# RWKV-7 block: the decay's copies to GpSimd, the inverse's transpose in two portions, and three edits to the order

## The chip, the cores and the metric

The kernel runs on one core of a Trainium2 chip. The metric is the device time of one execution in microseconds (us). Before the change it is 1290.84 us, the median of three runs (1290.55 to 1292.97).

A core has five engines, each with its own queue of instructions that it takes in order: TensorE (PE, matmul; its weight loads are shown apart as PEld), VectorE (DVE), ScalarE (ACT), GpSimd (POOL) and SyncE (SP), which here only issues DMAs. They wait for one another through semaphores. Matmuls write to PSUM, eight banks; all else lies in SBUF.

## The reference

Two layers over an input of 512 tokens by 1024 channels: an RG-LRU block with a gated convolutional FFN, then an RWKV-7 block with another. The change touches the RWKV-7 block alone:

```python
def _rwkv7_scan(r, w, k, v, aa, bb):
    ...
    def step(S, inp):
        r_t, w_t, k_t, v_t, a_t, b_t = inp
        sa = jnp.einsum('bhij,bhj->bhi', S, a_t)
        S = S * w_t[:, :, None, :] + sa[..., None] * b_t[:, :, None, :] + v_t[..., :, None] * k_t[..., None, :]
        y = jnp.einsum('bhij,bhj->bhi', S, r_t)
        return S, y
...
    decay = jnp.exp(-jnp.exp(w))
    a = jax.nn.sigmoid((a0 + (xa @ a1) @ a2).astype(f32))
    kk = (kf * k_k).reshape(bsz, seq, RWKV_H, RWKV_N)
    kk = kk / jnp.maximum(jnp.linalg.norm(kk, axis=-1, keepdims=True), 1e-12)
    kf = kf * (1.0 + (a - 1.0) * k_a)
    y = _rwkv7_scan(rh, hs(decay), kh, vh, -kk, kk * ah)
```

There are 16 heads of 64 channels. The state S of a head is 64 by 64 and depends on every token before.

## The kernel before

**Matmul precision.** Each float32 product is three matmuls (L54): both operands are split in a high part, rounded to the fast type, and a low part, the rest. For a weight, ACT makes the high part `wh` (L94) and DVE the low part `wl` (L97), each over 128x1024, some 1.0 and 1.2 us. For the mixed inputs `mix`, DVE makes both parts. Weights come by DMA, issued by SP.

**The scan in chunks.** The 512 tokens are cut into 8 chunks (NC) of 64 (C). Inside a chunk the recurrence becomes products of 64x64 matrices and the inverse of a triangular one. Blocks of 128 channels hold two heads; there are two groups of four blocks, g (or H) = 0 and 1.

- `prepare(g)` takes the decays, k and a of each block to the scaled operands. `pinv` (L1169) and `ppad` (L1172) are exponentials of the decays summed over the chunk, in the two directions, made by ACT. `ppad` is padded by one column per chunk and lies in two buffers, used in turn by the blocks. The r part of the tile AR is filled from `ppad` (L1183, 128x512): by ACT for g = 0, by DVE for g = 1. The last column of each chunk, the chunk's whole decay, goes to PC (L1187, 128x8), by ACT. DVE makes `kp` (L1180), the products with it (L1181, L1185, L1186), and ACT `sq` and `fac` (L1170, L1171). Then the norms of kk: `ssq` (L1179, PE), transposed as `sst` (L1194), reciprocals on DVE (L1198), transposed back as `rec` (L1202), split by ACT and DVE (L1204, L1205), spread to the channels by `knb` (L1211, PE) and multiplied in (L1212, DVE).
- `solve(H)` inverts the triangular 32x32 corners of all chunks at once. `aab` (L1281, PE) makes the corner matrices, DVE transposes them to A (L1294; in the second inverse A and its products D share a tile, shown as `DA`), POOL makes the identity X (L1297, L1298), and 31 steps of two DVE operations each (L1302, L1304) substitute. The result is transposed twice by DVE: to LT (L1307, 128x1024) and to XN (L1309). POOL copies LT's halves (L1313, L1314). `m1p` (L1328) and `ltp` (L1338), small PE products, complete it to 64x64.
- `rwkv_chunks` runs the steps over the chunks: masked products W (`s`, L1418, and L1425), `pe` (L1462), U from the inverse (`pu`, L1487; copied out by ACT, L1494), transposes of the keys (`tr`, L1432), the state (`pd`, L1481 and L1500), its decayed copy `tu` (L1507, DVE) and the output `py` (L1490, L1511).

**What sets the order.** The functions are generators. A projection calls `background(n)` after each small piece of its matmuls, and this advances a lane of generators by n visits, that is to their next `yield`. In the scan, `fill(i)` does the same from a table. The instructions that result are then ordered for each engine by a list scheduler with priorities and modelled durations; each engine executes in that order. `keep_in_program_order` (in `step` through `chained`) pins an instruction directly behind the one written before it on its engine. A `yield` more or less so moves what follows by one visit, and an operation given to another engine changes the order on both.

## Time and profile before

| | |
|---|---|
| time, median of 3 runs | 1290.84 us (1290.55 to 1292.97) |
| profiled execution | 1291.05 us, span 1289.3 us |
| busy: PE, DVE, ACT, POOL | 1264.2, 928.1, 642.8, 133.6 us |
| mean granted clock of PE | 0.997 |
| RWKV stage: prepare(0), first inverse, second inverse, rest of the scan | about 607 to 636, 650 to 705, 705 to 744, 744 to 890 us |

The profile is one execution. A row of the timeline has the start in us from the span's start, the time in us, the engine, line, operation, output and inputs, shapes, a count where equal instructions follow one another, and in brackets the time for which the engine had been idle and what ended it. Matmuls are pipelined: the time of one is longer than the distance to the next.

### The profile page before, as it was taken

How to read it: one execution, taken by the hardware profiler on the slowest of the kernel's cores; microseconds unless marked ns; L12 is line 12 of the kernel's file. 1: busy time of each engine (PE TensorE's matmuls, PEld its weight loads, DVE VectorE, ACT ScalarE, POOL GpSimd, SP SyncE). 2: the span in 40 equal slices, each digit the busy share in tenths (PEclk: the TensorE clock that was granted, in tenths of full speed). 3: DMA queues.
4: the chain of work that ended last, by engine and by line, in shares of the span. 5: the costliest groups of instructions: out<-in, count | busy, mean ns of one | idle time of the engine just before them, and what ended most of it. 6: DMA issues, size and time to landing. Idle time of an engine off the chain costs nothing. (4 is left out here: it accounts for less than half of the span.)

```text
span 1289.3 us, 22401 instructions
## 1 busy us (share of the span) xinstructions
PE 1264.2 (98%) x9259; PEld 1067.0 (83%) x9259; DVE 928.1 (72%) x1412; ACT 642.8 (50%) x1006; POOL 133.6 (10%) x206
## 2 busy tenths in 40 slices
PE   9999999999999999999899999999999999999998
PEld 8777888989898888877678888778889898988886
DVE  5998678757575766788999967778766566666653
ACT  6797455434343443559844346545644334343432
POOL 3000001010101010010002145410010101010100
PEclk9999999999999999999999999999999999999999
DMA  7312335455454544422212122132344454545431
GB/s 222 111 55 94 98 122 108 150 112 159 103 164 98 170 95 116 144 79 82 79 41 87 52 62 84 44 99 82 116 96 161 101 170 92 178 84 179 100 131 65
DMA packets 117829, 141.37 MB, mean 110 GB/s; under 512 B 10138, under 2 KB 91748, under 8 KB 117600
## 3 DMA queue, kind: packets, MB, share of 16 engines
q1 hardware_dynamic: 100528, 122.44, 29.8%
q0 software_dynamic: 16624, 16.47, 8.4%
q8 instruction: 72, 1.18, 0.4%
q10 hardware_dynamic: 576, 1.05, 0.2%
q14 instruction: 29, 0.24, 0.1%
HBM read 135.41 MB, written 4.52 MB: 109 GB/s over the span
## 5 line engine op out<-in xcount | busy, mean ns | idle before, releaser
L97 DVE TENSOR_TENSOR wl<-raw,wh 128x1024 fp32r<-128x1024 f32 (+1 forms) x161 | 194.4, 1213 | 124.7 <-ACT wh L94 104.0
L94 ACT CAST wh<-raw 128x1024 fp32r<-128x1024 f32 (+1 forms) x161 | 165.9, 1043 | 195.2 <-PE acc L54 56.0
L54 PE MATMUL accG<-xs,wh 128*128 128x512 f32 x448 | 138.7, 391 | 0.0
L54 PE MATMUL accU<-xs,wh 128*128 128x512 f32 x448 | 138.6, 391 | 0.0
L54 PE MATMUL acc<-hid,wh 128*128 128x512 f32 x384 | 119.8, 395 | 0.0
L744 DVE TENSOR_TENSOR lo<-raw,hi 128x1024 fp32r<-128x1024 f32 x70 | 85.5, 1222 | 39.4 <-PE accU L54 32.0
L743 ACT CAST hi<-raw 128x1024 fp32r<-128x1024 f32 x70 | 73.6, 1052 | 60.7 <-PE accU L54 25.3
L54 PEld LDWEIGHTS accG<-xs,wh 128*128 128x128 f32 x448 | 83.7, 188 | 17.3
L54 PEld LDWEIGHTS accU<-xs,wh 128*128 128x128 f32 x448 | 83.7, 188 | 17.2
L54 PE MATMUL accG<-xs,wl 128*128 128x512 f32 x224 | 87.3, 390 | 0.0
L54 PE MATMUL accU<-xs,wl 128*128 128x512 f32 x224 | 87.3, 390 | 0.0
L54 PEld LDWEIGHTS acc<-hid,wh 128*128 128x128 f32 x384 | 71.3, 187 | 16.7
L54 PE MATMUL accA<-xt,hi 128*128 128x256 f32 x480 | 83.4, 277 | 0.0
L54 PE MATMUL acc<-xs,wh 128*128 128x512 f32 x256 | 81.1, 398 | 0.0
L690 DVE SCALAR_TENSOR_TENSOR cv<-gpad,pv,cv 128x512 f32<-128x512 f32 x96 | 69.1, 748 | 12.3 <-ACT cv L688 11.8
L845 PE MATMUL acc<-wl,hid 128*128 128x512 f32 (+1 forms) x200 | 77.2, 386 | 0.0
L844 PE MATMUL acc<-wh,hid 128*128 128x512 f32 (+1 forms) x200 | 77.0, 385 | 0.0
L843 PE MATMUL acc<-wh,hid 128*128 128x512 f32 (+1 forms) x200 | 76.7, 383 | 0.0
L168 POOL DMA_DIRECT2D raw<-in_ffn_w_up_dram x20 | 25.7, 1285 | 480.8 <-DMA raw<-in_ffn_w_up_dram 336.3
L54 PE MATMUL acc<-hid,wl 128*128 128x512 f32 x192 | 75.0, 395 | 0.0
L54 PEld LDWEIGHTS accA<-xt,hi 128*128 128x128 f32 x480 | 73.2, 188 | 0.9
L54 PE MATMUL accA<-xt,lo 128*128 128x256 f32 x240 | 66.3, 276 | 0.0
(411 smaller groups left out, 2943.1 us busy)
## 6 DMA issues: line engine op xcount, KB each, us to landing
raw<-in_ffn_w_up_dram SPq DMA_DIRECT2D x106, 512.0 KB, 3.7
raw<-in_ffn_w_down_dram SPq DMA_DIRECT2D x48, 512.0 KB, 3.9
raw<-in_ffn_w_up_dram POOLq DMA_DIRECT2D x30, 512.0 KB, 5.9
raw<-in_rwkv_w_rkv_dram SPq DMA_DIRECT2D x24, 512.0 KB, 3.7
raw<-in_lru_w_in_dram SPq DMA_DIRECT2D x16, 512.0 KB, 4.3
raw<-in_lru_w_out_dram SPq DMA_DIRECT2D x8, 512.0 KB, 3.7
raw<-in_rwkv_w_out_dram SPq DMA_DIRECT2D x8, 512.0 KB, 3.6
xd<-x SPq DMA_DIRECT2D x8, 256.0 KB, 2.0
```

The source lines that it names most:

```text
L54: mm = lambda *a, **kw: self.nc.tensor.matmul(ps, *a, skip_group_check=more, **kw)
L94: put = (self.nc.vector.tensor_copy if dve else self.nc.scalar.copy)(hi, src)
L97: self.nc.vector.tensor_tensor(lo, src, hi.bitcast(F32), ALU.subtract)
L168: self.nc.gpsimd.dma_start(raw, more, accum_op=ALU.add)
L690: nc.vector.scalar_tensor_tensor(cv, pair.gp[:, e, j : j + T], cw(j), cv, ALU.mult, ALU.add)
L743: nc.scalar.copy(hi, f[p])
L744: tt(lo, f[p], hi.bitcast(F32), ALU.subtract)
L843: nc.tensor.matmul(ps, hh[:, s], wh[:, k, m], start=kk == 0, stop=False)
L844: nc.tensor.matmul(ps, hl[:, s], wh[:, k, m], start=False, stop=False)
L845: nc.tensor.matmul(ps, hh[:, s], wl[:, k, m], start=False, stop=kk == blocks - 1)
```

## The change

Five edits.

- The copies of r (L1183) and of the decay column (L1187) in `prepare` go to GpSimd for both groups: eight copies of 128x512, of which ACT made four and DVE four, and eight of 128x8, which ACT made.
- One more `yield` stands between `rec` and the `knb` loop.
- The transpose to LT is made in two halves of 16 columns; in the second inverse (H = 1) a visit lies between them.
- In the first inverse (H = 0) two visits instead of one lie between POOL's copies and `m1p`.
- In `step`, the second of U's two copies is pinned behind the first.

```diff
-                (nc.vector.tensor_copy if g else nc.scalar.copy)(rr, pp[:, :, :, 1:])
+                nc.gpsimd.tensor_copy(rr, pp[:, :, :, 1:])
                 self.done.add(("r", b))
                 nc.vector.tensor_tensor(Lc, ko, pp[:, :, :, 0:C], ALU.mult)
                 nc.vector.tensor_tensor(ko, bytok(kp), bytok(fac), ALU.mult)
-                nc.scalar.copy(PC[:, b, :], pad[:, :, C])
+                nc.gpsimd.tensor_copy(PC[:, b, :], pad[:, :, C])
                 yield 1
...
             nc.vector.tensor_tensor(rec[32:40], pr[32:40], rec[32:40].bitcast(F32), ALU.subtract)
+            yield 1
             yield 1
             for j in range(4):
...
-        nc.vector.transpose(LT[:, :, 0:32].rearrange("p u t -> p t u"), X)
+
+        for c in range(2):
+            nc.vector.transpose(LT[:, :, c * 16 : c * 16 + 16].rearrange("p u t -> p t u"), X[:, c * 16 : c * 16 + 16])
+            if H and c == 0:
+                yield 1
...
-        for _ in range(4 if H else 1):
+        for _ in range(4 if H else 2):
             yield 1
...
-            for g, bs, H, c, c2, q in gs:
+
+            for n_, (g, bs, H, c, c2, q) in enumerate(gs):
                 bh = half(1 - q)
-                nc.scalar.copy(uv[bh, bs], flat(pu[bh]))
+                chained(n_ == 0, nc.scalar.copy(uv[bh, bs], flat(pu[bh])))
```

Lines of the kernel after the change are one to six higher than before. What the edits move is best seen in three places.

ScalarE in `prepare(0)`, the difference of the two orders ( - is before, + is after). `wh` is the high part of a weight, `mt` a product for the mixed inputs.

```order
 L1169 ACTIVATE pinv<-AR_4902 128x512
-L1183 COPY AR_4902<-ppad_5254 128x4x2x64
-L1187 COPY PC<-ppad_5254 128x8
-L962 ACTIVATE mt<-x,om 128x512
 L1172 ACTIVATE ppad_5255<-AR_4902 128x8x64
 L94 CAST wh_5334<-raw_5262 128x1024
-L1171 ACTIVATE fac<-BK_4904,oka,pv 128x512
 L1170 ACTIVATE sq<-BK_4904,pv 128x512
 L1149 CAST back<-back 40x512
+L962 ACTIVATE mt<-x,om 128x512
 L1170 ACTIVATE sq<-BK_4904,pv 128x512
```

The two copies ahead of the cast are gone from this queue (two more pairs stood further ahead), and a multiplication for `mt` and a `fac` come behind the cast.

TensorE at the end of `prepare(0)`, the difference. `acc` are the projection's sums, `rec` and `knb` the norm's products.

```order
+L54 MATMUL acc_5261<-mix,wl_5398 128x512
 L1202 MATMUL rec<-ident,n_5218 40x128 x4
-L54 MATMUL acc_5261<-mix,wl_5398 128x512
-L1211 MATMUL knb<-rec,back 128x512 x4
+L1212 MATMUL knb<-rec,back 128x512 x4
 L54 MATMUL acc_5506<-early_4897,wh_5403 128x512 x2
```

The one matmul that stood between `rec` and `knb` stands ahead of both now.

VectorE at the end of the second inverse, before:

```order
L1304 TENSOR_TENSOR X<-X,DA 128x31
L1307 STREAM_TRANSPOSE LT_7154<-X 128x32x32
L1425 TENSOR_TENSOR W<-s,masks 128x512 x2
L97 TENSOR_TENSOR wl_6901<-raw_6646,wh_6900 128x1024
L1507 TENSOR_TENSOR tu<-pd,decay 64x256 x2
```

and after:

```order
L1305 TENSOR_TENSOR X<-X,DA 128x31
L1310 STREAM_TRANSPOSE LT_7155<-X 128x16x32
L1430 TENSOR_TENSOR W<-s,masks 128x512 x2
L97 TENSOR_TENSOR wl_6902<-raw_6647,wh_6901 128x1024
L1310 STREAM_TRANSPOSE LT_7155<-X 128x16x32
L1513 TENSOR_TENSOR tu<-pd,decay 64x256 x2
```

W stands behind half of the transpose instead of all of it, and the other half stands between the low part and `tu`. In the first inverse the first half moves up into the substitution, behind its step on 9x23 columns, and the second half stands where the whole transpose stood, with XN directly behind it. GpSimd's queue has the sixteen copies of `prepare` ahead of the identity of the first inverse; for its other work it keeps its order, but LT's copies of the second inverse stand behind the copies for one more step. On ACT, U's two copies stand next to each other in both orders.

## The prediction

> **What bounds the kernel now.** I read the page's first part, then TensorE's waits in the RWKV stage (600 to 890 us, the only stage that the change touches), then the windows and the timeline around the waits.

> ```profile
> span 1289.3 us, 22401 instructions
> PE 1264.2 (98%) x9259; PEld 1067.0 (83%) x9259; DVE 928.1 (72%) x1412; ACT 642.8 (50%) x1006; POOL 133.6 (10%) x206
> PE acc L54 <- ACT wh L94: 3.5, 2, 3.0
> PE pe L1462 <- DVE tu L1507: 2.6, 4, 1.1
> PE tr L1432 <- DVE W L1425: 1.5, 1, 1.5
> PE m1p L1328 <- DVE XN L1309: 1.2, 1, 1.2
> PE knb L1211 <- DVE rec L1205: 1.2, 1, 1.2
> ```

> TensorE (PE) is busy 1264.2 of 1289.3 us, so no change that leaves its matmuls as they are can win more than the 25 us that are left. The change adds and removes no matmul. It can win only the waits listed (columns: us in total, times, longest), some 10 us, and a slow clock that one of them brings. The profiled execution took 1291.05 us, 0.2 us over the median of the runs, 1290.84. The sum is made against 1291.05. A measurement of this kernel tells 0.2%, 2.6 us, from no change.

> ```profile
> 610.00:620.00 10.00, 6.98 (x27) 5.24 (x26) 10.00 (x18) 10.00 (x21) 0.00 (x0) 0.86 0.26 92
> 618.00:619.00 1.00, 1.00 (x4) 0.80 (x3) 1.00 (x2) 1.00 (x3) 0.00 (x0) 0.50 0.02 8
> 710.00:740.00 30.00, 28.17 (x548) 26.00 (x551) 27.97 (x68) 11.74 (x23) 3.35 (x9) 1.00 0.16 52
> 744.00:790.00 46.00, 45.59 (x1086) 41.91 (x1090) 31.29 (x48) 27.31 (x58) 23.27 (x33) 1.00 0.19 56
> ```

> The columns are length, busy time of PE, weight load, DVE, ACT and POOL, then the granted clock. In prepare(0), at 610 to 620, ACT and DVE are both busy for all 10.00 us while PE does 6.98. GpSimd (POOL) does nothing there. At 710 to 740 DVE, busy 27.97 of 30, carries the substitution. From 744 PE is full.

> **Part 1, r and the decay column to GpSimd.** PE's rows in prepare(0), and those of the engines that it waits for:

> ```profile
> 613.55 0.40 PE L54 MATMUL acc<-mix,wl 128*128 128x512 f32 x1
> 616.97 3.25 PE L54 MATMUL acc<-mix,wh 128*128 128x512 f32 x7 [3.02 <-ACT wh L94]
> 620.02 0.63 PE L54 MATMUL acc<-mix,wl 128*128 128x512 f32 x1
> 633.12 1.21 PE L1211 MATMUL knb<-rec,back 40*128 40x512 f32 x4 [1.16 <-DVE rec L1205]
> 615.89 1.03 ACT L94 CAST wh<-raw 128x1024 fp32r<-128x1024 f32 x1
> 614.13 0.60 ACT L1183 COPY AR<-ppad 128x512 f32<-128x512 f32 x1
> 614.64 0.20 ACT L1187 COPY PC<-ppad 128x8 f32<-128x8 f32 x1
> 614.74 0.72 ACT L962 ACTIVATE mt<-x,om 128x512 f32<-128x512 f32 x1
> 617.32 1.22 DVE L97 TENSOR_TENSOR wl<-raw,wh 128x1024 fp32r<-128x1024 f32 x1
> 627.95 0.20 DVE L1196 TENSOR_SCALAR n<-sst 128x32 f32<-128x32 f32 x1 [0.87 <-PE sst L1194]
> 630.47 0.41 DVE L1183 COPY AR<-ppad 128x512 f32<-128x512 f32 x1
> 630.80 0.69 DVE L1185 TENSOR_TENSOR AR<-BK,ppad 128x512 f32<-128x512 f32 x1
> 632.38 0.68 DVE L1205 TENSOR_TENSOR rec<-rec 8x512 fp32r<-8x512 f32 x1 [0.56 <-ACT rec L1204]
> ```

> PE stands 3.02 us for the weight's high part, which ACT casts at 615.89. Then the clock is halved: the row for 618 to 619 grants 0.50, and seven matmuls take from 616.97 to 620.02, 0.436 us each, twice their time at full clock: 1.5 us lost there and a little behind it, 1.6 in all. On ACT three r copies and three PC copies go from ahead of the cast (the last pair is quoted: 0.51 us to the next start, and 0.10), and one mix multiplication (the row at 614.74, 0.63 to the next) moves behind it: 3 × 0.61 + 0.63 = 2.5, so the cast starts near 613.4. That would cut the 3.02 to about 0.7.

> But what is late next is DVE. After eight high matmuls at 0.22 us PE needs the low part (L97), some 1.8 us after the cast's end at 614.5, and DVE has no gap up to it: of its work ahead, two operations (0.60 to the next start each, such as L1185) move behind it, so it starts at 617.32 − 1.2 and is ready about 617.3, some 1 us after PE asks. Further on, the rec row decides: knb follows rec directly in the new order, and rec is made on DVE. So the term is where L1205 starts. From 632.38 go three r copies that DVE no longer makes (0.33 of pitch each, 630.47 to 630.80) and two waits, 0.87 and 0.56, that an earlier PE closes: 632.38 − 1.0 − 1.4 = 629.95. knb came 0.74 behind L1205, so it would stand at 630.7 instead of 633.12: **2.4 us won if GpSimd's copies cost DVE nothing.** PE's other waits in this stretch are inside that number, because PE comes back to DVE's pace at knb.

> What do they cost DVE? No 128x512 copy on POOL is in this trace, so bounds come from its neighbours:

> ```profile
> L1441 POOL COPY tu<-x 64x256 f32<-64x256 f32 x32 | 16.0, 499 | 27.3 <-ACT x L1380 8.8 <-DVE XN L1309 5.4 <-DVE wl L97 4.7
> L1438 POOL COPY rts<-AR 64x128 f32<-64x128 f32 x32 | 12.5, 391 | 30.7 <-PE py L1490 18.3 <-PE pu L1487 11.1
> 714.39 0.39 POOL L1441 COPY tu<-x 64x256 f32<-64x256 f32 x1
> 781.06 1.73 POOL L1438 COPY rts<-AR 64x128 f32<-64x128 f32 x2
> 783.22 1.20 POOL L1441 COPY tu<-x 64x256 f32<-64x256 f32 x2
> 782.55 1.60 DVE L1565 TENSOR_TENSOR pr<-AR,BK 128x512 f32<-128x512 f32 x2
> 734.41 1.28 DVE L1565 TENSOR_TENSOR pr<-AR,BK 128x512 f32<-128x512 f32 x2
> ```

> From 64x128 to 64x256 a POOL copy grows by 108 ns per 128 elements of a row. Alone, as at 714.39, 64x256 takes 0.39; with 0.22 for 256 elements more, 128x512 takes some 0.6, an estimate. The engines also hold each other up: the pair L1565 takes 1.60 us beside POOL's copies (the two at 783.22 and the end of those at 781.06) and 1.28 without, so 0.32 us for two copies of 64x256, as many elements of a row as one r copy has. Six r copies stand ahead of rec, the four of block group 0 and two of group 1: 6 × 0.32 = 1.9. For the 128x8 copies I take 0.03 each, 0.2 for six (between nothing and 0.09). Then knb comes at 630.7 + 2.1 = 632.8, and **part 1 wins 0.3 us**. Bounds: 2.4 where a copy delays nothing, and where it holds DVE for its whole time, 6 × 0.6 = 3.6 and 0.1 for the small ones, the end is 634.4, a loss of 1.3. The value lies where it does because DVE has no gap at 610 to 620 in which a hold could hide. For the four copies that DVE made itself, 0.33 goes and 0.32 comes.

> [...]

> The clock should not fall again, since the longest new wait, 1 to 2 us, is shorter than the 3.02 that halved it; if it does, 1.6 is lost (third rival). What follows knb: the first product of the inverse (aab) now stands in four pieces between the projection's matmuls instead of three, and the four L1212 products run behind a low part and a mix multiplication, later by some 1.4 us of DVE: 0.1 lost, 0 to 0.4.

> **Extra visit ahead of knb, and the pin of U's copies.** rec and knb had one matmul between them and now have none, so the extra yield moves nothing that knb could hide behind: 0, with 0.23 (one matmul) as the end on the other side. U's copies already stood side by side on ACT, in that order: 0, and nothing queues anew.

> **First inverse's products one visit later.**

> ```profile
> 703.97 0.28 PE L1251 MATMUL acc<-wh,mix 128*128 128x256 f32 x1
> 704.09 0.28 PE L1252 MATMUL acc<-wl,mix 128*128 128x256 f32 x1
> 705.60 1.20 PE L1328 MATMUL m1p<-XN,O 32*32 32x32 f32 x64 [1.23 <-DVE XN L1309]
> 729.72 0.68 PE L1462 MATMUL pe<-tu,W 128*64 128x64 f32 x14 [1.07 <-DVE tu L1507]
> 738.20 0.69 PE L1462 MATMUL pe<-tu,W 128*64 128x64 f32 x16 [0.75 <-DVE tu L1507]
> 710.21 0.21 DVE L1302 TENSOR_TENSOR DA<-DA,X 128x31 f32<-128x31 f32 x1 [1.87 <-POOL X L1298]
> 741.86 1.95 DVE L1307 STREAM_TRANSPOSE LT<-X 128x1024 f32<-128x1024 f32 x1
> 743.67 1.25 DVE L1425 TENSOR_TENSOR W<-s,masks 128x512 f32<-128x512 f32 x2
> 747.07 0.86 DVE L1507 TENSOR_TENSOR tu<-pd,decay 64x256 f32<-64x256 f32 x2 [1.02 <-PE pd L1500]
> ```

> 24 more matmuls now stand ahead of m1p, 0.12 us apart (703.97 to 704.09), some 2.8 us, so its 1.23 goes. But PE then waits for DVE twice more, 1.07 and 0.75, for tu that DVE makes inside the second substitution. That chain begins at 710.21, released by POOL, not by PE, and ends with the transpose at 741.86 and W at 743.67. A PE that is 1.2 earlier at 707 waits 1.2 longer there. **0**, up to 1.2 if those waits don't grow. The first inverse's transpose in two halves, the first of them amid the substitution, costs one more start on DVE: 0.1 lost, 0 to 0.2.

> **Second inverse's transpose in halves.** PE's tr waits 1.46 us (the row of 1.5 in the waits) for W, which stood behind the whole 1.95 us. Now half lies ahead of it: W comes about 0.9 earlier. The second half runs after the next low part, in the 1.02 us in which DVE then waited for pd. **0.9 won**, 0.3 to 1.4. From 744 PE is full, so it stays won. Against it: in the later steps XN stands behind two W, m1p and ltp come later, and pd closes up to tr with two matmuls in between instead of six (four less at 0.12, some 0.5): 0.3 lost, 0 to 0.6.

> **Sum:** 0.3 − 0.1 + 0 + 0 − 0.1 + 0.9 − 0.3 = 0.7 us won, 1291.05 − 0.7 = **1290.4 us**.

> **The rivals.** R1, the copies are free: they run in parallel on an engine that is idle at 610 to 620. For it: the one pair that shows a delay met four short copies, each with a start of its own, and longer copies may hold less often. Against it: the 1.60 beside 1.28, and a DVE without a gap. Part 1 is 2.4 and the sum 2.8: 1288.2, and less where m1p's gain stays too.

> R2, the whole hold: every r copy takes its 0.6 from DVE. Part 1 loses 1.3, the sum is 0.9 on the other side: 1292.0. For it: DVE is busy without a gap in prepare(0). Against it: the measured 0.16 of 499 ns.

> R3, slower: the clock is halved again. With DVE behind by R2's hold, PE stands for the low part near 617 for over 2 us, and for rec for 2 us or more. From about 3 us of standing in one piece, as at 613.9 to 617, the clock falls and 1.6 us are lost: 1292.0 + 1.6 = 1293.6. Against it: the 1.46 at tr, with 1.00 granted in the windows on both sides.
> [...]

> R4, m1p's gain is kept: the waits for tu don't grow, since pe is asked for later by PE as well. 1290.4 − 1.2 = 1289.2.

> That the change doesn't do what it says holds for the pin and the extra visit; they are in the sum at 0.

> **How the numbers follow.** Forecast 0.38, R1 0.26, R2 0.14, R3 0.12, R4 0.10. The range from 1287.6 to 1293.2 holds the forecast's bounds, R1, R2 and R4, and leaves out most of R3 and the cases in which R1 and R4 fall together. R1's 1288.2 lies at the edge of faster by 0.2% (1288.26 from the median): I give two thirds of it to faster, with 0.08 for R1 or the forecast with R4's gain: 0.25. Slower: R3's 0.12. Within 0.2%: 0.63.

> **What would show it.** In the profile after: PE's wait for the high part at 614 is under 1 us and its place is taken by one for L97; the granted clock stays at 1.00; DVE's two-input rows in prepare are longer than 0.69 beside POOL's copies, by 0.3 a copy; knb stands near 632.8; m1p's wait is gone and the waits for tu are longer; tr's wait is near 0.6. I would be wrong if DVE's rows keep their length (R1), or if PE's granted clock falls in 610 to 640 (R3).

## The result, and the profile after

The changed kernel takes 1298.64 us, the median of five runs (1297.30 to 1300.01), against 1290.84 for the kernel before, measured alongside. The ratio is 1.0051, with a 95% interval of 1.0037 to 1.0066: slower by half a per cent, where 0.05% faster was forecast and the range ended at 1293.2. The profiled execution took 1297.30 us, 6.25 more than that of before.

The page of the changed kernel, its first lines:

```profile
span 1295.5 us, 22403 instructions
PE 1269.4 (98%) x9259; PEld 1070.3 (83%) x9259; DVE 931.6 (72%) x1410; ACT 639.1 (49%) x994; POOL 147.0 (11%) x222
```

Some of TensorE's waits in the changed kernel from 600 to 890 us (us in total, times, longest):

```profile
PE pe L1467 <- DVE tu L1513: 3.0, 3, 2.5
PE knb L1212 <- DVE rec L1205: 2.2, 1, 2.2
PE acc L54 <- ACT wh L94: 2.2, 2, 1.7
PE acc L54 <- DVE wl L97: 1.5, 2, 1.0
PE acc L1251 <- ACT ytok L1521: 0.8, 1, 0.8
PE tr L1437 <- ACT tu L1500: 0.5, 1, 0.5
PE tr L1437 <- DVE W L1430: 0.2, 1, 0.2
```

TensorE's waits are hardly longer in sum: of the span it is not busy for 26.1 us, against 25.1 before. What grew is its busy time, from 1264.2 to 1269.4 us, with the same 9259 matmuls. There are two sources of slower matmuls. The first shows in windows of one microsecond of the changed kernel (the eighth figure, PEclk, is the granted clock):

```profile
634.00:635.00 1.00, 1.00 (x4) 0.72 (x3) 0.97 (x2) 0.34 (x1) 1.00 (x3) 0.50 0.00 0
733.00:734.00 1.00, 1.00 (x29) 0.88 (x22) 0.90 (x4) 0.00 (x0) 0.00 (x0) 0.50 0.06 16
812.00:813.00 1.00, 1.00 (x16) 0.90 (x16) 0.97 (x2) 0.33 (x1) 0.00 (x0) 0.50 0.06 16
```

These are three spells at half clock, from 633.6, 732.6 and 811.1, each 3.41 us long, where the profile of the kernel before has one in this stage, at 617.1. TensorE is full in all three windows (busy 1.00 of 1.00 us at a clock of 0.50), so a spell costs up to 1.7 us, half its length, an estimate from these rows; it costs less where TensorE would have waited behind it in any case. The second source is in TensorE's timeline of the second inverse, first before, then after:

```profile
764.03 1.20 PE L1328 MATMUL m1p<-XN,O 32*32 32x32 f32 x64
767.75 1.20 PE L1328 MATMUL m1p<-XN,O 32*32 32x32 f32 x64
772.16 1.27 PE L1338 MATMUL ltp<-LT,M 32*32 32x32 f32 x64
776.07 1.20 PE L1338 MATMUL ltp<-LT,M 32*32 32x32 f32 x64
```

```profile
768.29 1.20 PE L1333 MATMUL m1p<-XN,O 32*32 32x32 f32 x64
771.46 0.66 PE L1437 MATMUL tr<-ident,BK 128*128 128x128 f32 x4 [0.46 <-ACT tu L1500]
774.04 0.39 PE L1251 MATMUL acc<-wh,mix 128*128 128x256 f32 x1 [0.84 <-ACT ytok L1521]
775.54 1.19 PE L1333 MATMUL m1p<-XN,O 32*32 32x32 f32 x32
777.21 1.19 PE L1333 MATMUL m1p<-XN,O 32*32 32x32 f32 x32
779.24 1.63 PE L1343 MATMUL ltp<-LT,M 32*32 32x32 f32 x64
782.54 1.60 PE L1343 MATMUL ltp<-LT,M 32*32 32x32 f32 x64
```

A product of two 32x32 matrices is two rows of the profile here, so `x64` is 32 products. Those of the second m1p take 1.20 us together before, and twice 1.19 after: in the changed kernel's order they stand in two blocks of 16 products, one for each q (0 or 1, which the kernel's `tile_position` puts on the lower or the upper 64 rows of the array). By the starts in the two timelines, two rows of the profile begin every 32 ns where the q alternate, and one where a block has one q. In ltp some products stand in such blocks and the others alternate, and it grows from 1.27 and 1.20 to 1.63 and 1.60. That is 1.9 us, and two new waits stand beside it, 0.46 and 0.84.

Where the 6 us arose is read from the start of the same TensorE instruction in both traces (after minus before, worked out from the timelines): −0.3 at 590; −0.7 at knb (632.40 against 633.12); +1.1 at 640, behind the first spell; +1.8 at 700; +0.5 at 721, since m1p's wait is gone; +3.35 at 737, behind the longer wait for tu and the second spell; +1.3 at 746, behind tr; +1.7 at 762; +5.0 at 800, behind the small products; +5.9 at 816, behind the third spell, and it hardly changes to the end.

From 640 to 746 VectorE passes the delay on. TensorE first loses more time near 697, at a wait for a low part. The second substitution then starts at 711.89, 1.68 later than before, and ends with the first half of the transpose and W, for which TensorE waits at tr:

```profile
696.49 0.39 PE L1253 MATMUL acc<-wl,mix 128*128 128x256 f32 x1 [0.43 <-DVE wl L97]
711.89 0.21 DVE L1303 TENSOR_TENSOR DA<-DA,X 128x31 f32<-128x31 f32 x1 [1.73 <-POOL X L1299]
744.02 1.08 DVE L1310 STREAM_TRANSPOSE LT<-X 128x512 f32<-128x512 f32 x1
744.95 1.26 DVE L1430 TENSOR_TENSOR W<-s,masks 128x512 f32<-128x512 f32 x2
```

So tr starts when W allows, 1.3 later than before, and most of what the second spell had cost by 737 is taken back there.

### The profile page after: what moved, and what is told of

The parts are those of the page before. It is cut to its first block, busy times and chain, and to the rows that moved or that the text cites. A ratio compares the mean times of both kernels' runs of the same rounds, so it can differ in the third digit from the quotient of the medians.

```text
span 1295.5 us, 22403 instructions
## 1 busy us (share of the span) xinstructions
PE 1269.4 (98%) x9259; PEld 1070.3 (83%) x9259; DVE 931.6 (72%) x1410; ACT 639.1 (49%) x994; POOL 147.0 (11%) x222
## 4 chain that ended last, share of the span: by engine, by line
PE 84%; DVE 9%; ACT 3%; issue 2%; POOL 1%; DMA 0%; POOLq 0%; ACTq 0%; DVEq 0%
PE acc L54 26%; PE accU L54 12%; PE accG L54 12%; PE accA L54 9%; PE accF L54 4%; PE acc L845 3%; PE acc L844 3%; PE acc L843 3%; PE accD L54 2%; DVE wl L97 1%; PE s L1423 1%; DVE X L1305 1%; DVE mt L965 1%; PE pe L1467 1%; PE pd L1506 1%
## 5 line engine op out<-in xcount | busy, mean ns | idle before, releaser
L97 DVE TENSOR_TENSOR wl<-raw,wh 128x1024 fp32r<-128x1024 f32 (+1 forms) x161 | 194.9, 1216 | 129.8 <-ACT wh L94 106.4
L94 ACT CAST wh<-raw 128x1024 fp32r<-128x1024 f32 (+1 forms) x161 | 165.9, 1042 | 193.3 <-PE acc L54 52.6
L54 PE MATMUL accG<-xs,wh 128*128 128x512 f32 x448 | 138.8, 391 | 0.0
L54 PE MATMUL accU<-xs,wh 128*128 128x512 f32 x448 | 138.6, 391 | 0.0
L54 PE MATMUL acc<-hid,wh 128*128 128x512 f32 x384 | 119.7, 394 | 0.0
L54 PEld LDWEIGHTS accG<-xs,wh 128*128 128x128 f32 x448 | 83.7, 188 | 17.4
L54 PEld LDWEIGHTS accU<-xs,wh 128*128 128x128 f32 x448 | 83.6, 188 | 17.2
L54 PE MATMUL accG<-xs,wl 128*128 128x512 f32 x224 | 87.3, 390 | 0.0
L54 PE MATMUL accU<-xs,wl 128*128 128x512 f32 x224 | 87.3, 390 | 0.0
L54 PEld LDWEIGHTS acc<-hid,wh 128*128 128x128 f32 x384 | 71.2, 187 | 16.7
L54 PE MATMUL accA<-xt,hi 128*128 128x256 f32 x480 | 83.4, 277 | 0.0
L54 PE MATMUL acc<-xs,wh 128*128 128x512 f32 x256 | 81.1, 398 | 0.0
L54 PE MATMUL acc<-hid,wl 128*128 128x512 f32 x192 | 74.9, 394 | 0.0
L54 PEld LDWEIGHTS accA<-xt,hi 128*128 128x128 f32 x480 | 73.1, 188 | 0.9
L54 PE MATMUL accA<-xt,lo 128*128 128x256 f32 x240 | 66.3, 276 | 0.0
```

Source lines behind the costliest of these rows:

```text
L54: mm = lambda *a, **kw: self.nc.tensor.matmul(ps, *a, skip_group_check=more, **kw)
L94: put = (self.nc.vector.tensor_copy if dve else self.nc.scalar.copy)(hi, src)
L97: self.nc.vector.tensor_tensor(lo, src, hi.bitcast(F32), ALU.subtract)
```

## The experiments

Theory S: each edit has a price of its own, the halves the largest. Rival P: GpSimd's hold on VectorE carries the loss. Rival C: the half clock alone is the loss. The kernel before spreads in the runs of the experiments from 1289.93 to 1296.77 us with a median near 1292.5, so each ratio is taken against runs of the kernel before that were measured alongside.

**One edit alone.** The pin of U's copies leaves the order of every engine row for row as it was, so it was not run by itself.

```diff
# e1: r and decay column to GpSimd
+                nc.gpsimd.tensor_copy(rr, pp[:, :, :, 1:])
+                nc.gpsimd.tensor_copy(PC[:, b, :], pad[:, :, C])
# e2: the transpose in halves
+        for c in range(2):
+            nc.vector.transpose(LT[:, :, c * 16 : c * 16 + 16].rearrange("p u t -> p t u"), X[:, c * 16 : c * 16 + 16])
+            if H and c == 0:
+                yield 1
# e3: one visit more
+        for _ in range(4 if H else 2):
# e4: a second yield between rec and knb
+            yield 1
```

> Only the r and decay-column copies go to GpSimd; the rest is as before. Theory S (each edit has a price of its own, and most of the loss is the second inverse's small products and VectorE's place for the halves): within 1291.05 +- 1.5, knb at 632.4 as in the changed kernel (0.7 earlier than 633.12), and 1.7 more where the halved clock falls on the stretch behind knb. Rival P (the copies on GpSimd hold VectorE and carry the loss): 1295 or more, with VectorE's rows in prepare longer by 0.3 a copy and nothing after 650 regained. Rival C (the clock alone is the loss): the granted clock falls to 0.5 near 633 as in the changed kernel, and the total is 1.5 over before.

> Only the transpose to LT in two halves, with the visit between them in the second inverse. Theory S: slower by 2.5 to 4 us, made of 0.7 at 695 (PE waits for a low part behind the half transpose), 1.0 for the second inverse's m1p in two pieces of 16 and 0.9 for its ltp at 22 ns instead of 16 ns a matmul, against 1.2 won at tr. Rival P: within 1 us of before. Rival C: no more than before but for 1.5 us where the clock falls in 720 to 740 or at 811.

> Only the one visit more ahead of the first inverse's m1p. Theory S: m1p's wait of 1.23 goes and the waits for tu grow by the same, 0 in all (1290 to 1291.5); where the clock falls behind the longer wait at 729, 1.5 more. If m1p's gain is kept instead: 1289.6. Rival P: as before. Rival C: slower by 1.5 with a clock of 0.5 at about 730 to 736.

> Only the second yield between rec and knb. Theory S: 0.2 lost at most, the one matmul that stood between them is now ahead of both, so knb's wait is 1.4 instead of 1.16: 1290.8 to 1291.5. If the sst transposes in one piece matter, the waits of VectorE for them change and knb comes at another time than 633.1. Rival C: 1.7 won where the wait at 614 falls otherwise on the clock's windows, and nothing else.

Measured, as ratios to before: e1 1.0017 (1.0005 to 1.0029), e2 1.0040 (1.0027 to 1.0053), e3 1.0003 (0.9991 to 1.0015), e4 1.0006 (0.9994 to 1.0018). The halves carry most, some 5 us where Theory S had 2.5 to 4, and GpSimd's copies the rest; the other two can't be told from nothing. The sum, 0.66%, covers the 0.51% of the whole. Rival P falls as the main cause. In e2 the small products are as slow as in the changed kernel, which ties them to that edit; the wait for a low part at 695, which Theory S put there, is not in e2. e1's profiled execution took 1292.60 us, 1.55 over that of before, with knb at 632.6 and the clock halved from 634.1: Theory S allowed 1.7 for that spell, and Rival C expected just this, so e1 alone does not part them. e2 does, since the clock explains no slow products there; in e4 knb's wait stayed 1.2 us and a wait for a low part near 698 was new (0.42). It stands in the changed kernel, in e7 and in e8 too (0.42 to 0.43, near 697), but in none of e1, e2 and e3, so the second yield brings it.

**The halves: the visit or the halving, and the overlap.** e5 takes the visit out. e6 keeps it and pins the products so that the two q alternate.

```diff
# e5
         for c in range(2):
             nc.vector.transpose(...)
-            if H and c == 0:
-                yield 1
# e6: halves with the visit, and in both loops of small products
+                    pin(u + q == 0, nc.tensor.matmul(pvs[q][hi[q], u, :], ...))
```

> The transpose to LT in halves for both inverses, without the visit between them; the rest is as before. TensorE's order is that of before, row for row, and VectorE still has W ahead of the second half. Theory V (the visit costs, since it sends m1p and ltp to another place among the projection's matmuls): tr's wait is 0.9 instead of 1.5, m1p at 764 to 768 keeps 16 ns a matmul, no wait of acc for ytok: 0.5 us faster than before, 0.9995 to 1.0. Rival H (two halves in themselves cost, on VectorE or GpSimd): slower as the halves with the visit, 1.003 or more.

> The halves with the visit, and each matmul of m1p and ltp pinned behind the one written before it, so that the two rows of the array alternate again. Theory Q (two thirds of the loss in the second inverse is the overlap of the two rows that is gone: m1p 2 x 1.0 us instead of 1.0, ltp 2 x 1.44 instead of 2 x 1.0): m1p and ltp back at 16 ns a matmul, about 1.9 us less than the halves with the visit, ratio 1.002 to 1.003. Rival W (the waits and the half clock behind them carry it): ratio unchanged at 1.004, though the small products are back at 16 ns.

Measured: e5 0.9998 (0.9986 to 1.0009), e6 1.0013 (1.0002 to 1.0024). So the halving costs nothing and the visit inside it does: without the visit, TensorE's order is that of before, tr's wait is 0.88 instead of 1.46, and there is no loss. The forecast 0.5 us gain of e5 is too small for these runs to show. In e6's timeline the small products of the second inverse overlap again:

```profile
776.68 0.24 PE L1332 MATMUL m1p<-XN,O 32*32 32x32 f32 x2
777.64 1.19 PE L1332 MATMUL m1p<-XN,O 32*32 32x32 f32 x62
779.68 1.19 PE L1342 MATMUL ltp<-LT,M 32*32 32x32 f32 x62
782.91 1.19 PE L1342 MATMUL ltp<-LT,M 32*32 32x32 f32 x62
```

62 of the 64 rows in 1.19 us (the first product stands apart). The ratio fell from 1.0040 to 1.0013, more than the 1.9 us of Theory Q; its forecast of 1.002 to 1.003 lies partly inside the interval. The clock makes up the rest: the mean granted clock was 0.9939 over the runs of e2 and 0.9963 over those of e6, against 0.9955 and 0.9953 for the kernel before beside them, and among the runs of the kernel before 0.001 less goes with some 0.7 us more. With that taken off, e2 is 4.0 us slower than the kernel before and e6 2.0, estimates from the runs' times and clocks, and the difference is Theory Q's. Rival W, no change, falls. What is left of e6's loss fits the two waits (0.84 for ytok is in its trace too), but that share was not tested.

**The other edits together.**

```diff
# e7: the whole change without the halves
# e8: the whole change, with
-        for _ in range(4 if H else 2):
+        for _ in range(3 if H else 2):
```

> The whole change without the halves. Theory S (prices add): ratio 1.002 to 1.003 (GpSimd 1.0017, visit 1.0003, second yield 1.0006), most of it as half-clock spells behind knb near 633 and behind pe near 731, while m1p's wait of 1.23 is gone. Rival J (the edits cost only together): 1.004 or more.

> The whole change, but with three visits instead of four ahead of the second inverse's m1p, so that the visit inside the transpose is taken back there. TensorE's order is that of the kernel without the halves, row for row. Theory V: 0.9 less than without the halves, since W comes 0.9 earlier: ratio 1.0015 to 1.0025. Rival H: as the whole change, 1.005.

Measured: e7 1.0017 (1.0006 to 1.0028), e8 1.0014 (1.0003 to 1.0024), against 1.0051 for the whole change. Giving back the visit ahead of m1p undoes over two thirds of the loss, so Rivals J and H fall. e7 lies a little under the 1.002 of Theory S, and e8 does not differ from e7 by what the runs can tell, though its tr waits 0.2 where e7's waits 1.0. Both profiles have spells at half clock near 633 to 634, 732 to 733 and 807 to 808.

**GpSimd's copies and the clock.** knb comes earlier with them, and still e1 is slower. The suspect was the spell behind knb's wait. e9, e10 and e11 fill that wait with eight matmuls whose result knb overwrites; e12 and e13 do the same with matmuls that use all 128 rows of the array instead of 40.

```diff
                 pb = self.bank("knb")
# e9 (with e1's edit), e10 (with e5's), e11 (with both)
+                for _ in range(8 if g + j == 0 else 0):
+                    nc.tensor.matmul(pb, backs[0][:, 0:P], backs[0], start=True, stop=True)
# e12 (with e1's edit), e13 (with e1's and e5's)
+                for _ in range(8 if g + j == 0 else 0):
+                    nc.tensor.matmul(pb, self.early[0][:, 0, 0, 0:P], self.early[0][:, 0, 0, :], start=True, stop=True)
```

> The copies on GpSimd alone, with eight matmuls ahead of knb whose result knb overwrites: 8 x 0.22 = 1.8 of the 2.2 us in which TensorE stands for rec. Nothing else moves on any engine. Theory C (GpSimd's edit costs by the half-clock spell that the longer wait at 630 brings, when TensorE is full behind it): no half clock at 633 to 638 in the profile, ratio 0.9985 to 1.0003, at least 1.5 us under the copies alone (1.0017). Rival P (the copies cost by holding VectorE, or later): the ratio stays at 1.0015 or more though the clock holds.

> The kernel before with the halves without the visit, and the eight matmuls ahead of knb. Theory C: the kernel before pays for spells behind its own wait for rec in some executions (0.5 at 634 in some profiles with before's order there), so the ratio is 0.998 to 0.9995 and the spread of runs is smaller. Rival: the eight matmuls take 1.8 where TensorE waits 1.16 only, so 0.6 is lost and the ratio is 1.000 to 1.0005.

> The copies on GpSimd, the halves without the visit, and the eight matmuls ahead of knb: the parts that lose nothing by the theories. Theory C: knb 0.5 earlier than before, W 0.9 earlier, no spell behind knb: 1.4 us and the spells of before saved, ratio 0.997 to 0.9995. Rival P: 1.001 to 1.002.

Measured: e9 1.0012 (1.0000 to 1.0025), e10 1.0008 (0.9992 to 1.0023), e11 0.9998 (0.9989 to 1.0006). e11 lies between the ranges of Theory C and of Rival P. Theory C as it stood falls: the wait is filled, and the clock is halved all the same, at 633 to 636 in all three profiles. The windows of e11:

```profile
630.00:633.00 3.00, 2.79 (x13) 1.88 (x11) 2.94 (x6) 3.00 (x6) 1.43 (x3) 1.00 0.52 175
634.00:635.00 1.00, 1.00 (x3) 0.81 (x3) 0.97 (x2) 0.41 (x1) 1.00 (x2) 0.50 0.00 0
```

TensorE stands for 0.21 us in the three ahead of the spell. So either the spell comes behind a filled wait because the eight matmuls use only 40 rows, or it has its cause earlier. Two more runs part these.

> The copies on GpSimd alone, with eight matmuls ahead of knb as in the first filled kernel, but with all 128 rows of the array in use instead of 40. Their result is overwritten; no other order moves. Theory A (a window of 3.41 us counts by the use of the array, so that 40-row matmuls count little and a spell at half clock followed though TensorE stood only 0.2 us): no spell at 633 to 638, ratio 0.9985 to 1.0005. Rival F (the spell at 633 follows five windows behind the wait at 614 to 617, whatever TensorE does at 630): the spell at 633 stays and the ratio is 1.001 to 1.002 as for the copies alone.

> The copies on GpSimd, the halves without the visit, and the eight matmuls of 128 rows ahead of knb. Theory A: no spell at 633 in the profile, fewer in all than before, ratio 0.998 to 0.9998. Rival F: the spell at 633 stays and the ratio is 0.9995 to 1.0005, as with the 40-row matmuls.

Measured: e12 0.9992 (0.9982 to 1.0002), e13 0.9982 (0.9969 to 0.9994). The same stretch in e13:

```profile
630.00:633.00 3.00, 2.60 (x14) 1.86 (x12) 2.94 (x6) 3.00 (x6) 1.42 (x3) 1.00 0.55 165
634.00:635.00 1.00, 1.00 (x6) 0.79 (x5) 0.97 (x2) 0.57 (x2) 1.00 (x2) 1.00 0.00 0
```

The clock stays at 1.00, though TensorE stands longer (0.40 us) than in e11. The eight matmuls take the same time, first in e11, then in e13:

```profile
630.16 2.10 PE L1212 MATMUL knb<-back 40*128 40x512 f32 x8
630.13 2.09 PE L1213 MATMUL knb<-early 128*128 128x512 f32 x8
```

They differ in the rows in use and in the values in them; the values were not varied by themselves. Theory A's forecasts hold here, where Rival F's fall; how the clock weighs the rows is Theory A's own reading and was not shown. e12 against e1 is 1.0017 to 0.9992 with that one edit, and the mean clock of the runs rose from 0.995 to 0.998.

That GpSimd's 0.17% is the price of the spell behind knb fits this, but it is not shown. e1's profiled execution, with one spell in this stage, is the fastest of its twelve, with a clock of 0.998, and does not show where the others lose. The kernel before was not run with the eight matmuls, and its own rows bring such a spell too: e2, e3, e5 and e6 have its rows up to 690 us, and all four have one from 634 to 636, behind 1.1 to 1.2 us of standing. The window of 635 to 636, in the profile of before and in that of e2:

```profile
635.00:636.00 1.00, 1.00 (x13) 0.56 (x15) 1.00 (x3) 0.90 (x2) 0.00 (x0) 1.00 0.52 199
635.00:636.00 1.00, 1.00 (x4) 0.80 (x3) 1.00 (x3) 0.85 (x2) 0.00 (x0) 0.50 0.51 199
```

e13 beats the kernel before by 0.2%: the copies on GpSimd, the halves without the visit, and eight matmuls that compute nothing. Seven of its eleven runs had a mean clock of 0.999, where most runs of before had 0.995 to 0.997. How much of this the eight matmuls alone would win in the kernel before is open.

## Why the prediction was wrong

**Right: the price of GpSimd's copies on VectorE, and, in part by luck, knb.** Forecast were 0.32 us a copy and knb at 632.8. Rows of the changed kernel's timeline, on VectorE, GpSimd and TensorE:

```profile
607.63 1.10 DVE L1185 TENSOR_TENSOR AR<-BK,ppad 128x512 f32<-128x512 f32 x1
611.07 0.68 DVE L1180 TENSOR_TENSOR kp<-BK,pinv 128x512 f32<-128x512 f32 x1
608.72 0.62 POOL L1183 COPY AR<-ppad 128x512 f32<-128x512 f32 x1
621.57 3.77 POOL L1183 COPY AR<-ppad 128x512 f32<-128x512 f32 x1 [5.46 <-ACT ppad L1172]
632.40 1.19 PE L1212 MATMUL knb<-rec,back 40*128 40x512 f32 x4 [2.24 <-DVE rec L1205]
```

The two-input operation beside a copy (L1185 at 607.63) takes 1.10 where one without takes 0.68 (L1180 at 611.07): 0.42 a copy. Ahead of rec there are six such delays, of 0.35 to 0.44, 2.4 us in all instead of the 2.1 forecast. The copy takes 0.62 at its shortest there, as estimated, so the whole hold of the second rival (0.6) is too much and free copies (the first) too little. knb stood at 632.40, earlier than forecast though VectorE lost more; 0.3 of that this execution was already ahead at 590. TensorE's wait for the high part fell from 3.02 to 1.7, not to 0.7, since the cast came at 614.29 instead of 613.4; knb was bound by VectorE, as forecast, so this cost nothing. Not foreseen: one copy lasted 3.77 us, beside a VectorE without gaps.

**Right: m1p.** Its wait of 1.23 went, and the wait for tu grew from 1.07 to 2.47. Nothing stayed won, which speaks against the fourth rival; e3 shows the same, within its interval.

**Right: W, though tr gained less.** W starts 0.93 us behind the start of the transpose instead of 1.81, 0.9 earlier as forecast. tr's wait fell from 1.46 to 0.22, but in part because TensorE came later: with the halves as the only edit it is 0.88 (e5) and 0.89 (e2), 0.6 less.

**Wrong: "The clock should not fall again, since the longest new wait, 1 to 2 us, is shorter than the 3.02 that halved it".** The waits became 2.24 and 2.47 us, and spells followed both, the first from 633.6 (a clock that falls in 610 to 640 was the prediction's own sign of being wrong); a third followed at 811 behind 1.76 us of standing in the 3.4 us ahead of it, worked out from the timeline. The 3.02 was taken for a threshold when it was only one case. The third rival was the right mechanism at the right place, with one spell for 1.6 us instead of three, and too little weight; it asked for the whole hold and for about 3 us of standing, and neither was needed.

**Wrong, and the larger: "in the later steps XN stands behind two W, m1p and ltp come later [...] 0.3 lost, 0 to 0.6".** It priced the later place by the matmuls that leave the gap between pd and tr, and put nothing for how the small products run in it. It measured 3.3 us, of which 1.9 in small products that no longer alternate, and 1.3 in waits for ACT (0.46 and 0.84). The order of TensorE shows the second m1p in two pieces of 16 products with three matmuls between; the prediction did not weigh that the pieces of one q lose their partner. This step and the clock make most of the distance from 1290.4 to 1298.6.

**Wrong, but small: the extra visit ahead of knb at 0.** It brings the wait of 0.43 for a low part near 697, behind which TensorE's delay grows from 1.1 to 1.8.

The median of before that the forecast was compared with, 1290.84, is a low draw: in the experiments the same kernel had medians of 1292.4 to 1292.9.

## What to carry to other kernels

In this kernel a wait of TensorE had two prices: its length, and up to 1.7 us more (half of a spell's 3.41, an estimate) where the clock was halved behind it. The second was paid where TensorE was full behind the wait, as at 811: the delay against the kernel before went from 5.0 to 5.9 us there and stayed. It was mostly not paid where TensorE waited again soon in any case: behind the spell at 617 knb waits 1.16 us for VectorE (the kernel before), and behind the one at 732 tr waits 0.22 us for it, and the delay went back from 3.35 to 1.3 us (the changed kernel). So a total of waiting that hardly changes, here 25.1 and 26.1 us, doesn't say that the time won't. And "later, on an engine that is full" was not free for small matmuls: 64 rows of m1p took 1.20 us with the two q alternating, and 2.38 in two blocks. Look whether their pairs still alternate in the new order, or pin them (e6: 62 rows in 1.19).

## What the runs showed of the hardware

The place and the length of the standing are not all. The kernel before and e2 ran the same rows up to 690 us and stood for the same 1.16 us in the same step, from 630.76, and only e2 had a spell behind it (a clock of 0.50 from 635 to 636, against 1.00). What decided there stays open.

In the wait ahead of knb, the rows in use made the difference, or the values in them, and not the time in which TensorE was busy: with eight matmuls on 40 rows it stood for 0.21 us from 630 to 633, and the clock was 0.50 from 634 to 635 (e11); with eight on 128 rows it stood for 0.40, and the clock was 1.00 (e13). A spell was also seen behind only 1.2 us of standing among 32x32 products near 708 (e12); whether the size of these products had a part in it was not tested.
